# Softmax attention of a hybrid trunk on transposed scores, with the row maximum carried in a 65th row of the operand

## The chip, the cores and the metric

The kernel runs on one core of one Trainium2 chip. Its engines are TensorE (matrix products; PE in the profile, its weight loads PEld), VectorE (DVE), ScalarE (ACT), GpSimd (POOL) and SyncE (SP, which issues the loads of the weights). The metric is the device time of one execution in microseconds; the time of a kernel is the median of its runs.

## What is computed

Two trunk layers work on 512 latent tokens and 256 context tokens of width 1024, in f32. Each layer projects the normalised tokens, feeds three groups of heads (mean pooling, bidirectional gated linear attention, softmax attention), concatenates their outputs, projects them, and ends in a squared-ReLU MLP. The change touches only the softmax attention:

```python
def gqa_attend(qb, k, v):
    s = jnp.einsum('bqhgd,bkhd->bhgqk', qb, k, preferred_element_type=jnp.float32) * HEAD_DIM ** -0.5
    p = jax.nn.softmax(s, axis=-1)
    return jnp.einsum('bhgqk,bkhd->bqhgd', p.astype(v.dtype), v)
...
    k_all = jnp.concatenate([kc_, kl], axis=1)
    v_all = jnp.concatenate([vc_, vl], axis=1)
```

There are 8 query heads of 64 and 2 key/value heads, each shared by 4 query heads. Latent queries see all 768 keys (256 of the context, 512 latent); context queries see the 256 context keys. In the second layer the context is not updated, so only the latent queries are computed there.

## The kernel before

**Formats.** A matrix is held as two parts, hi and lo, in a reduced f32 format (F32R); products add hi*hi, hi*lo and lo*hi. The attention's probabilities and values are multiplied in plain f32, which the trace shows as two matmul instructions for each matmul of the program.

**Order of the work.** The kernel is written with generators ("threads"): `gla_thread` for the gated linear attention, `a_thread` for the projections, `mods` for the modulation and `att_thread` for the softmax attention. The string STEPS says for each layer in which order they are advanced, one letter for a step (g, a, m, t); at a t the projections and the modulation are first run to their ends. After the string, `gla_thread` and then `att_thread` are run out. A planner then orders each engine's instructions by its own estimate of times, in which an instruction that stands earlier goes first if it is ready. So each engine's order is fixed when the program is built, and an engine that waits keeps everything behind it waiting.

**Buffers.** `slot` gives one of 33 shared buffers [128, 768] in SBUF; the weights' pool `wp` has 3 buffers "raw", 5 "hi" and 5 "lo" of 1024 columns, which the attention also uses. PSUM: `psA` two buffers of two banks, `psB` three of one bank, `psC` one of one bank.

**The attention** (lines 928 to 1059). `k_stack` transposes the keys and stacks them per kv head: kh holds the hi part twice (rows 0 to 63 and 64 to 127), kl the lo part twice. `q_stack(hp)` transposes the queries of a pair of heads hp (four pairs) and holds per head qs, hi above lo. A unit is two query tiles of 128 of one pair. `softmax_part` makes, for each of the unit's four (head, tile) cases, scores with the queries on the partitions, [128 queries, 768 keys], from kh and kl (L974, L975), in a psA buffer; VectorE takes the negated maximum along the keys (L977), ScalarE the exponential with that as bias, and the sum with it (L978). `value_part` takes, for each of six key tiles, four transposes of p on TensorE (L992), a copy out of PSUM on ScalarE or VectorE (L996, L998), and the product with the values for two heads, 256 columns each (L1001), added up in psC. At its end a product with the identity spreads the reciprocal sums over the partitions (L1008), VectorE multiplies (L1014), and the hi and lo parts of the result go to mixT. Context queries are a third unit of each pair in layer 0. In `att_thread` a unit's value part is interleaved with the next unit's softmax part, and one step of `pool_thread` follows each unit.

## Time and profile before

| what | value |
|---|---|
| median of 3 runs | 1718.49 us (1718.38 to 1723.11) |
| span of the profiled execution (its own time) | 1719.9 us, 1.4 us over the median |
| TensorE busy | 1639.1 us, 95% |
| VectorE, ScalarE, GpSimd busy | 866.9, 656.9, 480.3 us |
| mean granted TensorE clock | 0.980 |
| attention in layer 0 / layer 1 | from 222 to 388 us / from 1179 to 1306 us of the span |

Times are from the start of the span. In a group or a step of the timeline, "out<-in" names the tiles; a bracket gives the idle time before and what ended it. In a table by stretches each engine has its busy time and in brackets its number of instructions; then come the granted clock, the busy share of the DMA engines and GB/s. The busy time of matmuls counts overlapping ones once, while the mean duration of one is longer than the distance at which matmuls follow each other; distances are therefore taken from starts.

### The profile page before, as it was taken

How to read it: one execution, taken by the hardware profiler on the slowest of the kernel's cores; microseconds unless marked ns; L12 is line 12 of the kernel's file. 1: busy time of each engine (PE TensorE's matmuls, PEld its weight loads, DVE VectorE, ACT ScalarE, POOL GpSimd, SP SyncE). 2: the span in 40 equal slices, each digit the busy share in tenths (PEclk: the TensorE clock that was granted, in tenths of full speed). 3: DMA queues.
4: the chain of work that ended last, by engine and by line, in shares of the span. 5: the costliest groups of instructions: out<-in, count | busy, mean ns of one | idle time of the engine just before them, and what ended most of it. 6: DMA issues, size and time to landing. Idle time of an engine off the chain costs nothing.

```text
span 1719.9 us, 28685 instructions
## 1 busy us (share of the span) xinstructions
PE 1639.1 (95%) x12059; PEld 1337.3 (78%) x12059; DVE 866.9 (50%) x1209; ACT 656.9 (38%) x1136; POOL 480.3 (28%) x514
## 2 busy tenths in 40 slices
PE   7999797999999999999999999898899999999997
PEld 4988655669987887877888888696568888888885
DVE  4447758643543334333353454767764555445554
ACT  5445356662432113122131134646663432222222
POOL 1104535202301220312313263244312212222225
PEclk9999899999999999999999999898999999999999
DMA  9422340203343415334131222200014233333331
GB/s 309 131 85 75 136 161 3 100 27 122 111 138 96 153 50 184 120 94 147 50 122 56 68 89 75 72 2 2 2 74 130 79 99 98 99 98 98 98 98 49
DMA packets 140256, 163.38 MB, mean 95 GB/s; under 512 B 9412, under 2 KB 116304, under 8 KB 140128
## 3 DMA queue, kind: packets, MB, share of 16 engines
q1 hardware_dynamic: 133312, 147.10, 26.9%
q10 hardware_dynamic: 6816, 14.46, 2.3%
q8 instruction: 94, 1.54, 0.4%
q14 instruction: 34, 0.28, 0.0%
HBM read 157.31 MB, written 4.23 MB: 94 GB/s over the span
## 4 chain that ended last, share of the span: by engine, by line
PE 85%; DVE 5%; POOL 3%; DMA 2%; ACT 2%; issue 2%; SPq 0%; ACTq 0%; POOLq 0%; DVEq 0%
PE dn L291 25%; PE up L272 19%; PE op L291 7%; PE tm L291 6%; PE up L274 5%; PE fm L272 4%; PE av L1001 3%; PE pT L992 2%; PE pm L175 2%; PE up L281 2%; PE fm L274 2%; DMA rawm<-in_w_mod_dram 1%; PE sc L974 1%; PE att L722 1%; PE sc L975 1%
## 5 line engine op out<-in xcount | busy, mean ns | idle before, releaser
L144 ACT ACTIVATE whi<-raw 128x1024 fp32r<-128x1024 f32 (+2 forms) x182 | 184.8, 1031 | 582.2 <-PE dn L291 310.3
L1131 POOL TENSOR_TENSOR X<-X,rtmp 128x512 f32<-128x512 f32 x158 | 218.0, 1384 | 660.9 <-DVE rtmp L1130 660.6
L68 DVE TENSOR_TENSOR wlo<-raw,whi 128x1024 fp32r<-128x1024 f32 (+2 forms) x182 | 225.5, 1247 | 279.0 <-ACT whi L144 273.7
L291 PE MATMUL dn<-whi,ah 128*128 128x512 f32 x640 | 249.8, 390 | 0.4 <-DVE rtmp L1130 0.4
L291 PE MATMUL dn<-whi,al 128*128 128x512 f32 x640 | 249.1, 389 | 0.0
L291 PE MATMUL dn<-wlo,ah 128*128 128x512 f32 x640 | 246.8, 389 | 0.0
L1130 DVE TENSOR_TENSOR rtmp<-dn,ga 128x512 f32<-128x512 f32 x160 | 109.2, 689 | 231.4 <-PE dn L291 229.8
L272 PE MATMUL up<-h2h,whi 128*128 128x512 f32 x464 | 183.8, 396 | 0.7 <-ACT relu L1173 0.7
L272 PE MATMUL up<-h2l,whi 128*128 128x512 f32 x464 | 182.5, 393 | 0.0
L272 PE MATMUL up<-h2h,wlo 128*128 128x512 f32 x464 | 182.5, 393 | 0.0
L291 PEld LDWEIGHTS dn<-whi,ah 128*128 128x128 f32 x640 | 120.1, 188 | 29.8 <-ACT whi L144 4.2
L291 PEld LDWEIGHTS dn<-wlo,ah 128*128 128x128 f32 x640 | 120.1, 188 | 25.0
L291 PEld LDWEIGHTS dn<-whi,al 128*128 128x128 f32 x640 | 120.1, 188 | 24.5
L272 PEld LDWEIGHTS up<-h2h,whi 128*128 128x128 f32 x464 | 87.1, 188 | 31.4 <-ACT relu L1173 7.6
L272 PEld LDWEIGHTS up<-h2l,whi 128*128 128x128 f32 x464 | 87.1, 188 | 21.1 <-issue 1.7
L291 PE MATMUL tm<-whi,hTh 128*128 128x256 f32 (+1 forms) x352 | 102.6, 292 | 0.0
L272 PEld LDWEIGHTS up<-h2h,wlo 128*128 128x128 f32 x464 | 87.1, 188 | 19.6
L291 PE MATMUL tm<-whi,hTl 128*128 128x256 f32 (+1 forms) x352 | 101.3, 288 | 0.0
L291 PE MATMUL tm<-wlo,hTh 128*128 128x256 f32 (+1 forms) x352 | 100.5, 287 | 0.0
L291 PE MATMUL op<-whi,mixh 128*128 128x256 f32 x320 | 91.2, 285 | 0.9 <-ACT whi L144 0.9
L291 PE MATMUL op<-wlo,mixh 128*128 128x256 f32 x320 | 90.2, 284 | 0.3 <-DVE wlo L68 0.3
L291 PE MATMUL op<-whi,mixl 128*128 128x256 f32 x320 | 90.5, 283 | 0.0
(287 smaller groups left out, 3318.7 us busy)
## 6 DMA issues: line engine op xcount, KB each, us to landing
rawm<-in_w_mod_dram SPq DMA_DIRECT2D x80, 512.0 KB
raw<-in_w_up_dram SPq DMA_DIRECT2D x64, 512.0 KB
raw<-in_w_down_dram SPq DMA_DIRECT2D x64, 512.0 KB
raw<-in_w_in_dram SPq DMA_DIRECT2D x26, 512.0 KB
rawm<-in_w_mod_dram SPq DMA_DIRECT2D x32, 256.0 KB
raw<-in_w_out_dram SPq DMA_DIRECT2D x16, 512.0 KB
raw<-in_w_in_dram SPq DMA_DIRECT2D x12, 256.0 KB
ga<-gaD ACTq DMA_DIRECT2D x6, 512.0 KB
```

The costliest lines, as they stand in the source:

```text
L68: V.tensor_tensor(lo, full, hi.bitcast(F32), ALU.subtract)
L144: A.activation(hi, raw, AF.Copy)
L175: T.matmul(pm[32 * j:32 * j + 32, :], sstat[:, k, :], raw[:, (j % 2) * 512:(j % 2) * 512 + 512], start=(k == 0), stop=(k == KT - 1), skip_ ...
L272: T.matmul(ps[:, 0:NL], a, b[:, 0:NL], start=st, stop=sp_)
L274: T.matmul(ps[:, NL:NT], a, b[:, NL:NT], start=st, stop=sp_)
L281: T.matmul(ps[:, cs], a, b[:, cs], start=(k == 0 and i == 0), stop=(k == nk - 1 and i == 2))
L291: T.matmul(ps, a[:, sl], bb, start=(k == 0 and i == 0), stop=(k == nk - 1 and i == 2))
L722: T.matmul(ps[g * bw:(g + 1) * bw, o0:o0 + bw], xk[rows, j0:j0 + bw], xq[rows, i0:i0 + bw], start=True, stop=True)
L992: T.transpose(pt_[:, i * 128:(i + 1) * 128], p_[:, ki * 128:(ki + 1) * 128], ident)
L1001: T.matmul(av_[64 * hh:64 * hh + 64, 0:256], vst, pe[:, hh * 256:hh * 256 + 256], start=(ki == 0), stop=(ki == len(kts) - 1))
L1130: V.tensor_tensor(tmp, ps, ga[0 if t < 4 else 1][:, sl], ALU.mult)
L1131: (V if b == NB - 1 and not both and t == 3 else G).tensor_tensor(X[t][:, sl], X[t][:, sl], tmp, ALU.add)
```

## The change

The scores are made transposed, with the keys on the partitions, [128 keys, 512 queries], so that the exponentials come out in the layout in which the product with the values takes them.

- `k_stack`: kl keeps the lo part in rows 0 to 63 and gets a row of ones as row 64.
- `max_part(hp)` replaces `q_stack`: per head qs (hi and lo; for the second head of a pair with the halves exchanged) and a second operand qm (the hi part in rows 0 to 63, copied by GpSimd). Then scores with the queries on the partitions are made once more, from the hi parts alone (64 rows), for the maximum of each query (VectorE); the maxima of a pair are transposed by a product with the identity and put as row 64 of qm by ScalarE.
- `scores`: kh times qs, plus the first 65 rows of kl times qm. The row of ones times the row of negated maxima subtracts the maximum within the product; the exponential needs no bias.
- `lat_part(hp)`: six key tiles by two heads, each 512 queries wide; exponential into p; the product with the values, 512 columns per head, one key tile behind, into psC. The sums over the keys: GpSimd adds the p tiles (two additions of 1024 columns per head), VectorE the two halves, and in `weigh` a product with a column of ones adds over the partitions.
- `weigh`: the reciprocal by Ln and Exp on ScalarE and one correction on VectorE, then the hi and lo parts.
- `ctx_part(hp)`: the same for the context queries, in layer 0.
- `att_thread`: `max_part` of the next pair is interleaved with the current pair's parts; two steps of `pool_thread` follow each pair. STEPS is as before.

Two constants are added at the start: the identity in F32R, and `nmx`, zeroed, for the maxima. Comments and docstrings are removed as well.

```diff
+    identr = const.tile([128, 128], F32R, name="identr")
+    V.tensor_copy(identr, ident)
+    nmx = const.tile([128, 6, 33], F32R, name="nmx")
+    A.activation(nmx, ident[:, 0:1].unsqueeze(1).to_broadcast([128, 6, 33]), AF.Copy, scale=0.0)
...
-                G.tensor_copy(kl[64:128], kl[0:64].bitcast(F32))
+                A.activation(kl[64:65], ident[64:65, 64:65].to_broadcast([1, NT]), AF.Copy)
...
-        def softmax_part(n, hp, q0, P):
-        def value_part(n, hp, q0, P):
-        def q_stack(hp):
+        def max_part(hp):
+            mix_new(4 + hp)
+            pq = [psB("qT"), psB("qT")] if both else [psB("qT")]
             for t in live:
                 T.transpose(pq[t // 4][:, (t % 4) * 128:(t % 4 + 1) * 128], qview(t, hp), ident)
             for hh in range(2):
+                qs, qm = slot("qs", F32R), slot("qm", F32R)
+                hr, lr = slice(64 * hh, 64 * hh + 64), slice(64 - 64 * hh, 128 - 64 * hh)
                 for i, pq_ in enumerate(pq):
                     n0, n1 = (0, NL) if i == 0 else (NL, NT)
+                    src = pq_[hr, 0:n1 - n0]
+                    A.activation(qs[hr, n0:n1], src, AF.Copy)
+                    sub_lo(qs[lr, n0:n1], src, qs[hr, n0:n1])
+                G.tensor_copy(qm[0:64, 0:N_], qs[hr, 0:N_].bitcast(F32))
+                qst[2 * hp + hh] = (qs, qm)
+            yield
+            kh = kst[hp // 2][0]
+            for t in lat_tiles:
+                ps = [psA("mx"), psA("mx")]
+                for z0, zn in ((0, NL), (NL, NC)):
+                    for hh in range(2):
+                        hr = slice(64 * hh, 64 * hh + 64)
+                        T.matmul(ps[hh][:, z0:z0 + zn], qst[2 * hp + hh][0][hr, t * 128:(t + 1) * 128],
+                                 kh[hr, z0:z0 + zn], start=True, stop=True)
+                for hh in range(2):
+                    V.tensor_reduce(nmx[:, t, 32 * hh:32 * hh + 1], ps[hh][:, 0:NT], AX.X, ALU.max, negate=True)
+                yield
...
+            ps = psA("mT")
+            for t in live:
+                T.matmul(ps[0:33, t * 128:(t + 1) * 128], nmx[:, t], identr, start=True, stop=True)
+            for hh in range(2):
+                r0 = 32 * hh
+                A.activation(qst[2 * hp + hh][1][64:65, 0:N_], ps[r0:r0 + 1, 0:N_], AF.Copy)
+            yield
+        def scores(ps, hp, hh, kt, q0, qn):
+            kh, kl = kst[hp // 2]
+            qs, qm = qst[2 * hp + hh]
+            ks = slice(kt * 128, (kt + 1) * 128)
+            T.matmul(ps, kh[:, ks], qs[:, q0:q0 + qn], start=True, stop=False)
+            T.matmul(ps, kl[0:65, ks], qm[0:65, q0:q0 + qn], start=False, stop=True)
+        def weigh(hp, av, acc, q0, n):
+            sm = psB("sum")[:, 0:n]
+            for hh in range(2):
+                T.matmul(sm[64 * hh:64 * hh + 64], one.to_broadcast([128, 64]), acc[hh], start=True, stop=True)
+            r, u = slot("r", w=512)[:, 0:n], slot("u", w=512)[:, 0:n]
+            A.activation(r, sm, AF.Ln)
+            A.activation(r, r, AF.Exp, scale=-1.0)
+            V.scalar_tensor_tensor(u, r, -1.0, sm, ALU.mult, ALU.mult)
+            V.tensor_tensor(r, av, r, ALU.mult)
+            V.scalar_tensor_tensor(r, u, 2.0, r, ALU.add, ALU.mult)
+            mhi, mlo = mixT[4 + hp]
+            A.activation(mhi[:, q0:q0 + n], r, AF.Copy)
+            G.tensor_tensor(mlo[:, q0:q0 + n], r, mhi[:, q0:q0 + n].bitcast(F32), ALU.subtract)
+        def lat_part(hp):
+            av = psC("av")
+            P, acc = {}, []
+            pend = []
+            for kt in range(6):
+                for hh in range(2):
+                    if kt % 2 == 0:
+                        P[hh, kt // 2] = wp.tile([128, 1024], F32, tag="lo" if hh else "hi", name=nm("p"))
+                    s_ = psB("sT")
+                    scores(s_, hp, hh, kt, 0, NL)
+                    p_ = P[hh, kt // 2][:, (kt % 2) * 512:(kt % 2) * 512 + 512]
+                    A.activation(p_, s_, AF.Exp)
+                    pend.append((hh, kt, p_))
+                for hh, k_, p_ in pend[:-2]:
+                    T.matmul(av[64 * hh:64 * hh + 64, :], vview(k_, hp // 2), p_, start=(k_ == 0), stop=False)
+                pend = pend[-2:]
+                if kt == 3:
+                    for hh in range(2):
+                        acc.append(wp.tile([128, 1024], F32, tag="raw", name=nm("acc"), bufs=3))
+                        G.tensor_tensor(acc[hh], P[hh, 0], P[hh, 1], ALU.add)
+                yield
+            for hh, k_, p_ in pend:
+                T.matmul(av[64 * hh:64 * hh + 64, :], vview(k_, hp // 2), p_, start=False, stop=True)
+            for hh in range(2):
+                G.tensor_tensor(acc[hh], acc[hh], P[hh, 2], ALU.add)
+                V.tensor_tensor(acc[hh][:, 0:512], acc[hh][:, 0:512], acc[hh][:, 512:1024], ALU.add)
+            yield
+            weigh(hp, av, [a_[:, 0:512] for a_ in acc], 0, NL)
+            yield
...
         def att_thread():
             k_stack()
             yield
+            yield from max_part(0)
+            for hp in range(4):
+                nxt = max_part(hp + 1) if hp < 3 else iter(())
+                for part in (lat_part(hp), ctx_part(hp) if both else iter(())):
+                    for _ in part:
+                        next(nxt, None)
+                        yield
+                for _ in nxt:
+                    yield
                 next(pool_, None)
+                next(pool_, None)
             run(pool_)
```

More of the change, by code (lines that the diff above doesn't have):

```diff
@@ L1028, in q_stack @@
             for hh in range(2):
-                qs = slot("qs", F32R)
+                qs, qm = slot("qs", F32R), slot("qm", F32R)
+                hr, lr = slice(64 * hh, 64 * hh + 64), slice(64 - 64 * hh, 128 - 64 * hh)
                 for i, pq_ in enumerate(pq):
                     n0, n1 = (0, NL) if i == 0 else (NL, NT)
-                    src = pq_[64 * hh:64 * hh + 64, 0:n1 - n0]
-                    A.activation(qs[0:64, n0:n1], src, AF.Copy)
-                    sub_lo(qs[64:128, n0:n1], src, qs[0:64, n0:n1])
@@ L1035, in q_stack @@
-                qst[hp * 2 + hh] = qs
+                    src = pq_[hr, 0:n1 - n0]
[15 more added lines that the diff above has]
+                yield
@@ new lines, in max_part @@
+            if both:
+                ps = psA("mx")
+                for i in range(2):
+                    for hh in range(2):
+                        hr = slice(64 * hh, 64 * hh + 64)
+                        T.matmul(ps[:, hh * 512 + i * NC:hh * 512 + (i + 1) * NC],
+                                 qst[2 * hp + hh][0][hr, NL + i * 128:NL + (i + 1) * 128], kh[hr, NL:NT],
+                                 start=True, stop=True)
+                V.tensor_reduce(nmx[:, 4:6, 0:33:32].rearrange("p t h -> p h t"),
+                                ps.rearrange("p (h t k) -> p h t k", h=2, t=2), AX.X, ALU.max, negate=True)
+                yield
@@ new lines, in lat_part @@
+        def lat_part(hp):
[21 more added lines that the diff above has]
+                T.matmul(av[64 * hh:64 * hh + 64, :], vview(k_, hp // 2), p_, start=False, stop=True)
+            for hh in range(2):
+                G.tensor_tensor(acc[hh], acc[hh], P[hh, 2], ALU.add)
[3 more added lines that the diff above has]
+            yield
@@ new lines, in ctx_part @@
+        def ctx_part(hp):
+            av = psC("avc")[:, 0:NC]
+            ps, acc = [], []
+            for hh in range(2):
+                s_ = psB("sTc")
+                for i in range(2):
+                    scores(s_[:, i * NC:(i + 1) * NC], hp, hh, 4 + i, NL, NC)
+                p_ = slot("pcx", w=512)
+                A.activation(p_, s_, AF.Exp)
+                ps.append(p_)
+            yield
+            for i in range(2):
+                for hh in range(2):
+                    T.matmul(av[64 * hh:64 * hh + 64, :], vview(4 + i, hp // 2), ps[hh][:, i * NC:(i + 1) * NC],
+                             start=(i == 0), stop=(i == 1))
+            for hh in range(2):
+                acc.append(slot("accx", w=NC))
+                G.tensor_tensor(acc[hh], ps[hh][:, 0:NC], ps[hh][:, NC:512], ALU.add)
+            weigh(hp, av, acc, NL, NC)
+            yield
@@ L1039, in att_thread @@
             yield
-            q_stack(0)
-            yield
-            nonlocal nunits
-            units = [(hp, q0) for hp in range(4) for q0 in ((0, 2, 4) if both else (0, 2))]
-            nunits = len(units)
-            prev = iter(())
-            for n, (hp, q0) in enumerate(units):
-                P = []
-                for i, _ in enumerate(softmax_part(n, hp, q0, P)):
-                    for _ in range(2 if i < 2 else 1):
-                        next(prev, None)
+            yield from max_part(0)
[4 more added lines that the diff above has]
+                        next(nxt, None)
+                        yield
+                for _ in nxt:
                     yield
-                run(prev)
-                if q0 == 0 and hp < 3:
-                    q_stack(hp + 1)
-                prev = value_part(n, hp, q0, P)
                 next(pool_, None)
-                yield
-            yield from prev
+                next(pool_, None)
             run(pool_)
```

68 lines of the change are left out of this document (removed).

## The prediction

> **What bounds the kernel now.** I read the page first, then the busy time by stage, then single steps of the attention on the timeline, then the chain of waits at the stage's ends. The page's rows:
>
> ```profile
> span 1719.9 us, 28685 instructions
> PE 1639.1 (95%) x12059; PEld 1337.3 (78%) x12059; DVE 866.9 (50%) x1209; ACT 656.9 (38%) x1136; POOL 480.3 (28%) x514
> PE 85%; DVE 5%; POOL 3%; DMA 2%; ACT 2%; issue 2%; SPq 0%; ACTq 0%; POOLq 0%; DVEq 0%
> ```
>
> TensorE holds 85% of the chain that ended last. The chain in order of time shows where the attention starts (the keys' transposes) and where the output projection takes over in layer 0, and the same in layer 1:
>
> ```profile
> 222.46 0.81 PE kT L933 x6
> ...
> 387.97 37.10 PE op L291 x307
> ...
> 1179.08 0.66 PE kT L933 x6
> ...
> 1305.35 14.71 PE op L291 x121
> ```
>
> Busy time in these two stages, and in three stretches of them where the linear attention (the GLA thread) runs beside:
>
> ```profile
> core 0: us, PE busy (x) PEld busy (x) DVE busy (x) ACT busy (x) POOL busy (x), PEclk, DMA share, GB/s
> 222.00:388.00 166.00, 148.40 (x1777) 98.54 (x1773) 106.39 (x175) 103.91 (x232) 55.29 (x74) 0.96 0.19 68
> 1179.00:1306.00 127.00, 113.56 (x1253) 77.45 (x1252) 85.53 (x134) 84.06 (x177) 38.83 (x55) 0.95 0.14 50
> ...
> 240.00:260.00 20.00, 16.52 (x239) 11.76 (x238) 17.06 (x28) 15.07 (x30) 9.99 (x11) 0.91 0.05 15
> 260.00:280.00 20.00, 13.82 (x348) 9.17 (x349) 18.68 (x23) 14.34 (x30) 16.21 (x18) 0.83 0.02 4
> 1200.00:1220.00 20.00, 18.11 (x340) 11.09 (x339) 19.69 (x31) 16.63 (x39) 15.37 (x22) 0.91 0.01 3
> ```
>
> Over both stages TensorE is the bound (148 of 166, 114 of 127 us), with 17.6 and 13.4 us idle. In the stretches with GLA it is VectorE (18.7 and 19.7 of 20 us), GpSimd is near behind, and TensorE idles at a granted clock of 0.83 to 0.91. How much of the old work lies behind GLA's end, the transposes of p show:
>
> ```profile
> 222.00:318.00 96.00, 12.46 (x72) 8.14 (x72) 3.38 (x5) 6.80 (x12) 0.93 0.16 58
> 318.00:388.00 70.00, 24.30 (x153) 16.41 (x152) 7.62 (x12) 16.25 (x28) 1.00 0.23 82
> ...
> 1255.00:1306.00 51.00, 18.15 (x120) 12.82 (x120) 6.89 (x10) 11.59 (x20) 1.00 0.34 121
> ```
>
> 153 of 225 in layer 0, so 68%, run after 318 us, and 120 of 192 (62%) in layer 1 after 1255 us; there GLA's matmuls have ended, and only TensorE's sum of work counts.
>
> **The change, priced on TensorE.** I count per pair of heads (four pairs a layer). A step of the old value part, from one group of four transposes to the next, and a tile of the old scores:
>
> ```profile
> 336.49 0.40 PE L974 MATMUL sc<-kh,qs 128*128 128x512 f32 x1
> 336.72 0.39 PE L975 MATMUL sc<-kl,qs 128*128 128x512 f32 x1
> 336.95 0.28 PE L974 MATMUL sc<-kh,qs 128*128 128x256 f32 x1
> 337.06 0.28 PE L975 MATMUL sc<-kl,qs 128*128 128x256 f32 x1
> ...
> 355.09 0.65 PE L1001 MATMUL av<-pe,UV 128*64 128x256 f32 x4
> 355.67 0.66 PE L992 MATMUL pT<-ident,p 128*128 128x128 f32 x4
> 356.26 0.65 PE L1001 MATMUL av<-pe,UV 128*64 128x256 f32 x4
> ...
> 381.56 0.61 PE L1008 MATMUL rb<-ident,sm 128*64 128x128 f32 x8
> 382.00 0.60 PE L1001 MATMUL av<-pe,UV 128*64 128x256 f32 x4
> ```
>
> I take starts, since durations overlap: a step is 356.26 - 355.09 = 1.17 us, of which 0.58 is the f32 product for 256 columns on both heads (the trace shows each f32 matmul as two instructions). A matmul of 512 columns in the scores takes 0.23, one of 256 takes 0.12, so a tile is 2 x 0.23 + 2 x 0.12 = 0.70 us. The reciprocal sums take 0.44 us a unit.
> *Before, latent:* 8 score tiles 5.6, 12 steps 14.0, two rb groups 0.9: 20.5 us. *Context (layer 0):* 8 matmuls of 256 1.0, 2 steps 2.3, rb 0.4: 3.7 us. Layer 0: 4 x 24.2 = 96.8; layer 1: 4 x 20.5 = 82.0.
>
> *After.* The nearest row to an f32 product with 512 columns on two heads is the modulation's pair of 512-column f32 matmuls:
>
> ```profile
> 237.05 1.05 PE L175 MATMUL pm<-rawm,sstat 128*32 128x512 f32 x4
> 238.03 0.43 PE L756 MATMUL o<-AT,GU 128*64 128x128 f32 x2
> ```
>
> It occupies 0.98 us. Bounds: 0.86 (the 0.58 scaled without its fixed part, about 2 x 0.43) and 1.16 (twice 0.58); I take 0.98, the same shape. So a key tile costs 4 score matmuls x 0.23 + 0.98 + 0.1 for the change between the two formats = 2.0 us, 12.0 for six. The pass for the maxima (max_part) multiplies 64 rows per head. GLA's 64-row matmuls in the chain:
>
> ```profile
> 210.42 1.54 PE att L722 x93
> ```
>
> They start every 1.54 / 93 = 0.017 us, so two heads can share the array, there with 32 to 64 columns. Bounds for a query tile: 0.35 (fully shared) and 0.70 (one after the other); I take 0.55, as 128-column weight loads come in any case: 2.2 for four tiles. Transposing the maxima (mT) is six matmuls of at most 0.11 (a transpose step is 0.58 / 4 = 0.15 with its change of format): 0.7, in layer 1 0.4. The sums by a product with ones: 0.98. Latent: 15.9 in layer 0, 15.6 in layer 1. Context: 8 x 0.12 + 2 x 0.58 + sum 0.58 + maxima 0.24 = 2.9. Layer 0: 4 x 18.8 = 75.2; layer 1: 62.4.
> **Sum on TensorE:** 178.8 - 137.6 = 41.2 us less. Queries are transposed as before.
>
> **The other engines.**
>
> ```profile
> L996 ACT ACTIVATE pe<-pT 128x512 f32<-128x512 f32 x72 | 41.5, 597 | 22.3 <-PE pT L992 18.4 <-PE av L1001 3.4
> L977 DVE TENSOR_REDUCE nmx<-sc 128x1 f32<-128x768 f32 x64 | 60.5, 953 | 25.9 <-PE sc L975 25.5
> L1130 DVE TENSOR_TENSOR rtmp<-dn,ga 128x512 f32<-128x512 f32 x160 | 109.2, 689 | 231.4 <-PE dn L291 229.8 <-POOL X L1131 1.7
> L925 POOL TENSOR_TENSOR mixl<-pm,mixh 128x768 fp32r<-128x768 f32 x2 | 3.6, 1817 | 7.8 <-ACT mixh L924 7.8
> L925 POOL TENSOR_TENSOR mixl<-pm,mixh 128x512 fp32r<-128x512 f32 x2 | 2.6, 1284 | 4.0 <-ACT mixh L924 4.0
> ```
>
> ScalarE: twelve exponentials of 512 columns at 0.6 (L996) are 7.2 us a pair; with split, row copies, Ln and Exp under 15 of TensorE's 16 to 19: hidden. The copies of transposed p (72 x 0.6) go. VectorE: the 8 reductions stay (7.6 us); 2.75 us of pe copies a pair go, three operations at 0.69 and two half-sums come: no gain, no loss. GpSimd: four sums of 128x1024 a pair. From 512 to 768 columns a sum grows by 0.53 us, so 1024 take 1.82 + 0.53 = 2.35; 9.4 us a pair, 75 us in all, where 55 and 39 us were busy. It stays below TensorE, so no term in throughput.
>
> *Waits that come.* The value product keeps its one bank until weigh has read it. After the last exponential of a pair come two GpSimd sums 4.7, VectorE 0.7, the ones product 1.0, Ln and Exp 1.2, two VectorE operations 1.4: 9.0 us. Queued behind is the next pair's first value product and, in order behind that, all of TensorE; ScalarE's exponentials and VectorE's maxima wait for TensorE. Cover: the old pair's last two products (2.0) and the next pair's scores, 12 x 0.46 = 5.5 us, which need only score banks and p tiles. That is 7.5, and max_part steps lie between, so I price it at nothing where the scheduler puts scores ahead; without that cover see the slower rival. The qm tiles double what a pair holds of the 33 shared buffers; if max_part then starts late, up to 8 reductions (7.6 us) stand open per pair: 0 to 46 us for the six hand-overs, and I take 0, as emission runs one pair ahead.
> *GLA.* GpSimd's operations are already stretched when VectorE is busy:
>
> ```profile
> 243.81 0.83 POOL L704 TENSOR_TENSOR xk<-b 128x384 f32<-128x384 f32 x1
> ...
> 261.66 1.71 POOL L697 TENSOR_TENSOR xq<-b 128x384 f32<-128x384 f32 x1
> ```
>
> STEPS, whose letters stay, issues 26 attention steps among GLA's in either layer. In layer 0 that was 26 of about 65 steps and is now 26 of about 48, so about two pairs' sums (18.8 us a layer) fall among such operations. Bounds 0 and 18.8; GpSimd was nearly full in one 20 us stretch of the five that GLA takes, so I take a fifth, 4 a layer: plus 8. The Trainium skill, "SBUF — State Buffer", section "Who interferes with whom", says that VectorE with two SBUF inputs and GpSimd reading SBUF block each other for a whole instruction; the factor of 2 in the two rows agrees. By that rule taken to its end the 18.8 would be lost whole in both layers, and the sum would be 1719.9 - 41.2 + 37.6 = 1716.3.
> *The ends.* No DMA is added or moved on its queue, but in layer 0 the first weight of the output projection waits for a raw buffer:
>
> ```profile
> 381.82 3.76 DMA raw<-in_w_out_dram
> ...
> 385.60 1.06 ACT whi L144
> ```
>
> Now two of the three raw buffers carry the sums and one is free early; against that stands the last pair's 9 us. Bounds -6 and +9 a layer; I take 0. The constants at the start (one 128x128 copy, one activation): 0 to 1, taken 0.
>
> Forecast: 1719.9 - 41.2 + 8 = 1686.7 for the profiled execution; the runs' median stands 1.4 lower, so **1685 us**.
>
> **Rivals.**
> 1. *Forecast*, chance 0.52, own range 1670 to 1703 (maxima unshared +5, GLA 0 to +20, ends).
> 2. *Idle time goes too*, 0.17: score banks are freed by one reduction instead of reduction and exponential, so GLA gets them sooner and half of the 31 us idle goes: 1719.9 - 41.2 - 15.5 = 1663, by the runs 1662. For it: the idle lies in the GLA stretches. Against: VectorE at 19.7 of 20 there.
> 3. *The saving falls into the GLA stretch*, 0.12: only what lies behind GLA counts (68% of 21.6, and 62% of 19.6: 26.8), and GpSimd's sums stretch GLA by two thirds of their 18.8, 13 a layer, which the rows with twofold times make possible: 1720 - 26.8 + 26 = 1719, by the runs 1718. For it: the two GpSimd rows. Against: TensorE's total would have to leave 40 us idle.
> 4. *Slower: the single value bank*, 0.19. If the order puts the next pair's first value product after only two key tiles (1.8 us) and the old products (2.0), 9.0 - 3.8 = 5.2 us stand open in each of eight pairs, 42 us: even. With the sums stretched twofold, as in the rows above, 4.7 becomes 9.4 and 9.9 x 8 = 79 us stand open: 1719.9 - 41.2 + 79 + 8 = 1766. Midway, 1745. It decides from 5 us a pair. For it: a bank without a second buffer, sums on the slowest engine. Against: the order of today's steps shows products and transposes of other units filling such waits.
>
> **How the numbers follow.** Within 0.3% (5 us) a measurement of this kernel cannot be told from no change. Faster: 0.52 + 0.17 + 0.03 of rival 3 = 0.72; same 0.08; slower 0.20. Range: 1656 leaves out the best part of rival 2, 1728 the worse two thirds of rival 4; 1685 is the likeliest.
>
> **What would show it.** Right: value products in steps of about 2.0 us a key tile, no transposes of p, the two stages about 18 and 16 us shorter. Wrong: TensorE waiting for VectorE's or GpSimd's sums ahead of the first value product of a pair (rival 4); GLA ending over 10 us later (rival 3); max_part's heads starting 0.23 us apart (the unshared bound); a key tile well over 2.0 us.

## The result, and the profile after

The changed kernel takes 1812.67 us (median of 4 runs, 1809.57 to 1819.27) where the kernel before, run beside it, takes 1720.8 us: a ratio of 1.0533, 95% interval 1.0504 to 1.0562, so about 92 us slower. Forecast was 1685 us with a range of 1656 to 1728. Neither the forecast nor its range held.

The page after (its span and its busy times):

```profile
span 1810.2 us, 27365 instructions
PE 1696.6 (94%) x11459; PEld 1312.0 (72%) x11459; DVE 889.2 (49%) x1190; ACT 629.9 (35%) x1025; POOL 563.2 (31%) x558
```

TensorE is *busier* than before (1696.6 against 1639.1 us) with 600 instructions fewer. The chain in order of time shows that the attention of layer 0 begins where it did, and that GLA's last matmuls (rg) and the output projection (op) come far later; then layer 1:

```profile
221.49 0.81 PE kT L939 x6
...
350.54 1.93 PE rg L787 x16
...
435.87 4.94 PE op L296 x31
...
1232.45 0.65 PE kT L939 x6
...
1346.90 1.02 PE rg L787 x16
```

Busy time by stretch, from the keys' transposes to the first matmul of the output projection in each layer (columns as in the prediction: length, busy PE, PEld, DVE, ACT, POOL, granted clock, DMA). First the kernel before, then the one after:

```profile
222.00:387.00 165.00, 147.68 (x1772) 98.03 (x1769) 105.39 (x174) 103.30 (x231) 55.29 (x74) 0.96 0.19 67
1179.00:1302.00 123.00, 109.56 (x1223) 74.08 (x1221) 82.52 (x131) 82.46 (x175) 38.83 (x55) 0.94 0.12 44
```

```profile
221.00:434.00 213.00, 175.54 (x1448) 82.38 (x1443) 117.91 (x164) 87.56 (x158) 98.15 (x97) 0.83 0.16 54
1232.00:1387.00 155.00, 131.64 (x938) 59.51 (x937) 89.76 (x117) 68.66 (x130) 76.34 (x73) 0.80 0.08 28
```

The two stretches grew from 165 + 123 = 288 to 213 + 155 = 368 us, so 80 of the 90 us by which the span grew lie here. No engine is full in them. I split a stretch into three parts that add up to it: *idle* is its length less PE busy; *clock loss* is (1 - granted clock) times its length, which is what half clock costs if TensorE is busy throughout it (an estimate); *work* is the rest, TensorE's work as it would be at full clock. Sums over both layers, in us (the clock's two digits leave about 2 us open):

| kernel | length | idle | clock loss | work |
|---|---|---|---|---|
| before | 288 | 31 | 14 | 243 |
| after | 368 | 61 | 67 | 240 |
| forecast for after (and 8 for GLA) | 255 | 31 | 14 | 202 |

So three things went wrong at once: the work fell by 3 us and not by 41, the idle time doubled, and the clock loss rose by 53 us.

Where the work stayed is seen in layer 0 behind GLA's end. The timeline of TensorE (start, duration):

```profile
373.70 0.50 PE L1004 MATMUL sT<-qs,kh 128*128 128x512 f32 x1
...
374.38 1.07 PE L1037 MATMUL av<-p,UV 128*64 128x512 f32 x2
375.38 0.50 PE L1004 MATMUL sT<-qs,kh 128*128 128x512 f32 x1
...
377.05 0.61 PE L975 MATMUL mx<-kh,qs 64*128 64x512 f32 x2
377.59 0.50 PE L1004 MATMUL sT<-qs,kh 128*128 128x512 f32 x1
...
387.02 0.62 PE L975 MATMUL mx<-kh,qs 64*128 64x512 f32 x4
...
398.29 0.29 PE L1005 MATMUL sTc<-qm,kl 65*128 65x256 f32 x1
...
404.25 2.03 PE L1066 MATMUL avc<-pcx,UV 128*64 128x256 f32 x7 [4.67 <-ACT pcx L1061]
...
414.73 1.08 PE L1037 MATMUL av<-p,UV 128*64 128x512 f32 x4
...
416.87 1.08 PE L1037 MATMUL av<-p,UV 128*64 128x512 f32 x4
```

"x4" is the product of both heads (two instructions each), "x2" that of one head. Both last the same: 1.08 and 1.07 us. A key tile with the heads side by side takes 416.87 - 414.73 = 2.14 us (forecast 2.0). With the heads apart one *head* takes 375.38 - 373.70 = 1.68 us, so 3.36 a tile. Counted in the trace's order, 37 of the 96 latent value products stand alone between other work. The maxima's products do the same: their rows last 0.62 us for two heads together (x4) and 0.61 us for one head alone (x2). By starts, one head alone takes 377.59 - 377.05 = 0.54 us, and both heads side by side take 0.55 us (1348.98 to 1349.53 us, in layer 1).

Where the idle time came from: TensorE's three largest waits in layer 0's stretch, 21 of its 37 us of idle time (engine, line, releaser: us in total, times, longest), and what ScalarE did around one of the first kind:

```profile
PE avc L1066 <- ACT pcx L1061: 11.8, 3, 6.9
PE mx L975 <- DVE nmx L978: 4.8, 6, 1.7
PE sum L1011 <- DVE acc L1048: 4.3, 1, 4.3
```

```profile
399.61 0.60 ACT L1014 ACTIVATE r<-sum 128x512 f32<-128x512 f32 x1 [4.10 <-PE sum L1011]
...
403.08 0.63 ACT L1020 ACTIVATE mixh<-r 128x512 fp32r<-128x512 f32 x1 [2.21 <-DVE r L1018]
403.61 1.06 ACT L1061 ACTIVATE pcx<-sTc 128x512 f32<-128x512 f32 x2
```

The context's scores (sTc) were ready at 398.6 us. Their exponentials (pcx) stood in ScalarE's queue behind the latent weigh of the same pair (Ln, Exp, mixh), which waited for the sums; so they began at 403.61, 5 us late, with ScalarE idle for most of that time. TensorE's context product (avc) waited for them from 399.6 to 404.25, and all behind it waited too.

The end of layer 1, where nothing is left to cover the last pair's chain:

```profile
1379.96 1.03 PE L1045 MATMUL av<-p,UV 128*64 128x512 f32 x4
1385.55 1.97 PE L1011 MATMUL sum<-acc,one 128*64 128x512 f32 x2 [4.56 <-DVE acc L1048]
1387.44 0.58 PE L296 MATMUL op<-whi,mixh 128*128 128x256 f32 x1
```

### The profile page after: what moved, and what is told of

Same layout as the page of the kernel before. It is cut to its first block, busy times and chain, and to the rows that moved or that the text cites. A ratio compares the mean times of both kernels' runs of the same rounds, so it can differ in the third digit from the quotient of the medians.

```text
span 1810.2 us, 27365 instructions
## 1 busy us (share of the span) xinstructions
PE 1696.6 (94%) x11459; PEld 1312.0 (72%) x11459; DVE 889.2 (49%) x1190; ACT 629.9 (35%) x1025; POOL 563.2 (31%) x558
## 4 chain that ended last, share of the span: by engine, by line
PE 82%; DVE 6%; issue 4%; ACT 3%; POOL 3%; DMA 2%; ACTq 0%; POOLq 0%; SPq 0%; DVEq 0%
PE dn L296 23%; PE up L277 18%; PE tm L296 6%; PE op L296 6%; PE up L279 5%; PE fm L277 4%; PE av L1037 3%; PE pm L180 2%; PE up L286 2%; PE sT L1004 2%; PE fm L279 1%; DMA rawm<-in_w_mod_dram 1%; PE mx L975 1%; PE sum L1011 1%; DVE nmx L978 1%
## 5 line engine op out<-in xcount | busy, mean ns | idle before, releaser
L68 DVE TENSOR_TENSOR wlo<-raw,whi 128x1024 fp32r<-128x1024 f32 (+2 forms) x182 | 230.4, 1274 | 286.9 <-ACT whi L149 283.7
```

Source lines behind the costliest of these rows:

```text
L68: V.tensor_tensor(lo, full, hi.bitcast(F32), ALU.subtract)
```

## The experiments

Four theories at the start. **P**: products of one head alone cost as much as those of two. **W**: the chain of sums and weigh, behind one value bank or in the queues. **M**: the pass for the maxima. **C**: work that uses half of the array halves the clock. Each time is the median of a variant's runs (two of most, four of e20, one of e7); the ratio is to the kernel before, run beside it on the same chip, with its 95% interval. Where two variants are compared by their medians, the intervals leave about 10 us open, and more where the text says so.

### Heads bound together; sums left out; maxima left out

e1_pairs:

```diff
-    T.matmul(av[64 * hh:64 * hh + 64, :], vview(k_, hp // 2), p_, start=(k_ == 0), stop=False)
+    last = behind(T.matmul(av[64 * hh:64 * hh + 64, :], vview(k_, hp // 2), p_, start=(k_ == 0),
+                           stop=False), last)
```

(`behind` only fixes the order in TensorE's queue; `last` begins as the last score product.)

> The arithmetic of the changed kernel; only the order is bound: in lat_part the first value product of a key tile has to stand behind the last score of the next key tile, and the second head's product behind the first head's, so that most of the 96 products of head 0 stand next to those of head 1 (in the changed kernel 52 of 96 do). Theory P (products that stand apart cost twice and bring more changes of format): 30 to 50 us faster than the changed kernel, with the value products' own time on TensorE falling from 76 towards 50 us. Theory W (the weigh chain behind one value bank): within 10 us of the changed kernel, since sums and bank are as they were. Theory M (the pass for the maxima): within 10 us too. Theory C (half clock brought on by products that use half of the array at a time): as P in time, and the time at a granted clock of 0.5 in the two attention stages falls well below the 136 us of the changed kernel.

e2_nogsum:

```diff
-G.tensor_tensor(acc[hh], P[hh, 0], P[hh, 1], ALU.add)
...
-G.tensor_tensor(acc[hh], acc[hh], P[hh, 2], ALU.add)
-V.tensor_tensor(acc[hh][:, 0:512], acc[hh][:, 0:512], acc[hh][:, 512:1024], ALU.add)
+V.tensor_tensor(acc[hh][:, 0:512], P[hh, 2][:, 0:512], P[hh, 2][:, 512:1024], ALU.add)
```

> Leaves out GpSimd's four 128x1024 sums of each latent pair of heads, so that the denominators hold two of six key tiles only; scores are divided by 8 in the exponential so that nothing overflows (same instructions). Theory W: the waits of the weigh chain shrink by the sums' 5 us or more per pair, eight pairs: about 40 us faster than the changed kernel, or more where GLA's GpSimd operations were stretched (the GLA end in layer 0 back by 15 us of its 37). Theories P, C and M: less than 10 us faster, since TensorE's products and their order stay.

e3_nomax: max_part keeps the queries' part; the loop of mx, nmx and mT goes, and

```diff
-A.activation(qst[2 * hp + hh][1][64:65, 0:N_], ps[r0:r0 + 1, 0:N_], AF.Copy)
+A.activation(qst[2 * hp + hh][1][64:65, 0:N_], ident[64:65, 0:1].to_broadcast([1, N_]), AF.Copy)
```

> Leaves out the whole pass for the maxima (its matmuls, VectorE's reductions and the transposes of the maxima); the 65th row is zero and scores are divided by 8 in the exponential, so that nothing overflows. The pass was forecast at 2.2 to 3.1 us a pair on TensorE, some 21 us in all. Theory M (the pass costs far more than that, by its waits on the two banks and VectorE, and at half clock): 50 us or more faster than the changed kernel. Theories P and W: 15 to 25 us faster, the forecast price.

e5_pairs_nomax, both of these edits:

> Both edits: no pass for the maxima (65th row zero, scores divided by 8 in the exponential) and the value products of the two heads bound together. Theory P and M together: the sum of the two gains, 80 us or more faster than the changed kernel, so faster than the kernel before. If pairing gains only because the pass for the maxima stands between the two products, the two gains overlap and this run is less than 10 us ahead of the run without maxima alone. Theory C: with no 64-row products left, granted clock near 1.0 in layer 0 after GLA's end.

| kernel | us | ratio | us against the changed kernel |
|---|---|---|---|
| e1_pairs | 1819.61 | 1.0556 (1.0511 to 1.0602) | +7 |
| e2_nogsum | 1773.54 | 1.0289 (1.0212 to 1.0366) | -39 |
| e3_nomax | 1778.88 | 1.0320 (1.0273 to 1.0367) | -34 |
| e5_pairs_nomax | 1782.48 | 1.0341 (1.0298 to 1.0383) | -30 |

```profile
224.00:435.00 211.00, 169.39 (x1430) 80.91 (x1427) 114.65 (x163) 87.59 (x157) 98.78 (x97) 0.81 0.16 55
1234.00:1398.00 164.00, 138.91 (x939) 64.77 (x937) 87.66 (x116) 68.89 (x130) 76.91 (x73) 0.72 0.08 27
```

These are e1's stretches. Its work fell by 18 us (240 to 222, by the same split), which confirms what theory P says of the price; yet idle rose to 67, clock loss to 86, and the time did not fall (the 7 us more cannot be told from none). So P's work is real, and TensorE's work does not set the end. Leaving out the sums gave W's 39 us, though GLA's end, counted from the keys' transposes, came back by 9 us only, not 15. M's 34 us lie between the two expectations. By e3's stretches TensorE's work fell by 40 us, where the prediction priced the pass at 23:

```profile
224.00:419.00 195.00, 154.75 (x1335) 74.22 (x1330) 94.46 (x128) 86.79 (x158) 102.85 (x97) 0.79 0.17 59
1216.00:1355.00 139.00, 107.50 (x859) 47.50 (x857) 70.00 (x84) 67.64 (x130) 79.48 (x73) 0.85 0.09 31
```

(idle 72, clock loss 62, work 200). In e5 the gains did not add; binding the heads gained nothing there either, and the clock did not come back to 1.0 as theory C had it (0.78 in both stretches).

### The bank, the sums and the clock

e6_free (weigh), e8_late (lat_part, weigh; the context likewise), e9_free_late (both):

```diff
+avs = slot("avs", w=512)[:, 0:n]
+A.activation(avs, av, AF.Copy)
```

```diff
-G.tensor_tensor(acc[hh], acc[hh], P[hh, 2], ALU.add)
 V.tensor_tensor(acc[hh][:, 0:512], acc[hh][:, 0:512], acc[hh][:, 512:1024], ALU.add)
+V.tensor_tensor(acc[hh][:, 0:512], acc[hh][:, 0:512], P[hh, 2][:, 0:512], ALU.add)
-weigh(hp, av, [a_[:, 0:512] for a_ in acc], 0, NL)
+weigh(hp, av, [(acc[hh][:, 0:512], P[hh, 2][:, 512:1024]) for hh in range(2)], 0, NL)
```

> The arithmetic of the changed kernel; weigh first copies the value product from its bank to a shared buffer (one ScalarE copy, 0.6 us, for latent and context each), so that the bank comes free about 1 us after the last product and not at the end of the chain of sums. Theory W-bank (the next product stands behind the held bank): TensorE's 11.8 us of waits of the context products in layer 0 go, and with them part of the half clock: 20 to 40 us faster than the changed kernel. Theory W-sums (the length of GpSimd's sums is the cost, wherever they end): less than 8 us. Theory P (products apart) and M (maxima): less than 8 us.

> The same result with other sums: only the last key tile is left to the end. GpSimd adds four key tiles as before, VectorE (two operations of 512 columns a head) the halves of that and the fifth tile, and the product with ones takes the rest in a second accumulating step (about 1 us of TensorE a pair); in the context the product with ones takes both tiles and GpSimd's sum goes. Theory W-sums: most of the 39 us that leaving out the sums gave, less 8 us of TensorE: 20 to 35 us faster than the changed kernel. Theory W-bank: 10 to 25 us, since the bank is held for a shorter time. Theories P and M: 8 us slower (TensorE's added steps).

> Both edits: the bank freed by a copy, and the late sums. If held bank and long sums are one and the same wait, the gains overlap and this run is within 8 us of the better of the two; if they are two costs, the gains add up, to 45 us or more below the changed kernel (1767 us or less).

e6: 1816.2 us (1.0534, 1.0504 to 1.0565), e8: 1802.88 us (1.0457, 1.0423 to 1.0491), e9: 1817.26 us (1.0541, 1.0510 to 1.0571). With the bank freed early, TensorE waits for the same exponentials as long as before (waits of e6, layer 0):

```profile
PE avc L1069 <- ACT pcx L1064: 12.2, 3, 7.2
```

The bank was not the wait that ended last: that part of theory W falls. Shorter sums (e8) gave 10 us, half of what theory W-sums asked for at least, and nothing together with the copies: e9 met neither of its two expectations; why not, no run shows.

e7_clock (the kernel before, and behind its last output):

```diff
+def val(hh):
+    mm(ps[64 * hh:64 * hh + 64, 512:1024], m32[:, 0:64], m32)
...
+for _ in range(28):
+    val(0)
...
+for _ in range(18):
+    mx(0)
+    full(2)
+    val(0)
...
+for _ in range(28):
+    val(0)
+    val(1)
```

> The kernel before with some 250 us of TensorE work behind its last output, issued back to back with no waits, so that each kind's granted clock can be read: whole-array matmuls of 512 columns (0.23 us each) around five stretches of about 28 us: one head's f32 value product over and over; one head's 64-row product as in the pass for the maxima; the mixture of the changed kernel (64-row product, two whole-array ones, one head's value product); both heads' value products in turn; both heads' 64-row products in turn. Theory C (half of the array in use at a time is enough to halve the clock): granted clock near 0.5 in the first three stretches, near 1.0 in the last two and in the whole-array stretches. Rival (only waits of TensorE halve it): near 1.0 in all of them, one head's value product about 1.0 us, 64-row products 0.23 us apart.

The timeline of TensorE, with rows run together where the operation stays the same; then busy time and granted clock: one row near the start, and one each within the stretches of one head's value products, of 64-row products (with whole-array ones around) and of the mixture:

```profile
1716.49 23.53 PE L1213 MATMUL mic<-mr 128*128 128x512 f32 x90 [8.10 <-ACT mr L1208]
1739.95 24.25 PE L1213 MATMUL mic<-m 128*64 128x512 f32 x56
...
1818.03 1.07 PE L1213 MATMUL mic<-m 128*64 128x512 f32 x2
...
1820.11 1.07 PE L1213 MATMUL mic<-m 128*64 128x512 f32 x2
...
1868.33 24.25 PE L1213 MATMUL mic<-m 128*64 128x512 f32 x112
```

```profile
1720.00:1730.00 10.00, 10.00 (x40) 8.10 (x39) 0.00 (x0) 0.00 (x0) 0.00 (x0) 0.87 0.00 0
...
1740.00:1763.00 23.00, 23.00 (x55) 7.40 (x55) 0.00 (x0) 0.00 (x0) 0.00 (x0) 1.00 0.00 1
1765.00:1818.00 53.00, 53.00 (x231) 42.27 (x229) 0.00 (x0) 0.00 (x0) 0.00 (x0) 1.00 0.00 1
1819.00:1853.00 34.00, 34.00 (x83) 11.08 (x83) 0.00 (x0) 0.00 (x0) 0.00 (x0) 1.00 0.00 0
```

Theory C falls as it was stated: with no waits the clock stays at 1.00 in one head's value products, in 64-row products and in their mixture. Half clock follows waits: after 8.1 us without work TensorE started at half clock. But e7 enters each of these stretches at full clock, so it does not test a weaker form of C: that such work is slow to lift a clock that has fallen. No run tests that. A stretch of the kernel after speaks for it: behind a wait of 3.62 us the clock stayed at 0.50 for 22 us in which TensorE was busy throughout.

```profile
263.93 0.66 PE L957 MATMUL qT<-ident,Uq 128*128 128x128 f32 x2 [3.62 <-ACT p L1034]
```

```profile
265.00:287.00 22.00, 22.00 (x163) 8.24 (x162) 11.36 (x12) 9.83 (x22) 10.90 (x9) 0.50 0.00 1
```

In the traces' record the clock changes only at steps of 3.41 us. Counted there, over both stretches: of the steps at half clock in which TensorE was busy throughout, full clock followed on 5 of 5 in the kernel before, but on 10 of 23 in the kernel after.

Theory P's price is confirmed in the cleanest form: 28 value products of one head take 24.2 us (x56, 0.86 us each), and 28 of *two* heads take the same 24.2 us (x112). The mixture shows what it costs to change between these products, in format and in the part of the array that they use: a cycle (one value product, one 64-row product, two whole-array ones) takes 1820.11 - 1818.03 = 2.08 us, where its parts alone are 0.86 + 3 x 0.23 = 1.55, so 0.53 a cycle.

### The order of emission

e11_defer: a pair's context scores come first, the value products are copied out of their bank, and weigh is called late:

```diff
+avs = held(av, NL)
...
-weigh(hp, av, [a_[:, 0:512] for a_ in acc], 0, NL)
+left.append(lambda: weigh(hp, avs, [a_[:, 0:512] for a_ in acc], 0, NL))
...
+if kt in (1, 3) and left:
+    left.pop(0)()
```

> The same arithmetic and the same GpSimd sums in another order of emission: a pair's context scores and exponentials come ahead of its latent ones, its context product and a copy of it (0.6 us) behind the first latent tile, and weigh (sums product, Ln, Exp, normalising) of a pair is emitted only behind the second key tile of the next pair. Theory W-order (the chain's steps stand in the engines' in-order queues ahead of work that is ready: in the changed kernel the context's exponentials waited on ScalarE behind the latent weigh, and TensorE behind those): the waits of 4 to 7 us per pair behind GLA's end go, and with them half clock; 30 to 50 us faster than the changed kernel. Theory P (the lone products and changes of format fill TensorE): less than 10 us. Theory G (the attention's steps among GLA's stretch GLA, and that sets the end): less than 15 us.

e12_half_t: every second t of STEPS left out from the third on.

> The changed kernel with 14 instead of 26 attention steps issued among GLA's in each layer (every second letter t left out; the rest follows behind GLA). Theory G: GLA's end comes back by 20 us or more of its 37 in layer 0 and its 39 in layer 1, and the whole is 15 to 40 us faster than the changed kernel. Theory W-order: GLA's end comes back, but what is moved behind GLA meets the same waits; within 10 us of the changed kernel, or slower by up to 20.

e13_defer_late is e11 with e8's sums; e14_defer_late_half is that with e12's STEPS.

> The deferred order of the run before last and the late sums (GpSimd adds four key tiles, VectorE the fifth, the product with ones takes the last in a second step). Theory W-order: with the weigh chain out of the way, GpSimd's sums have no one waiting for them, so within 8 us of the deferred order alone. If GpSimd's sums cost by their share of GLA's GpSimd work or VectorE's: 10 us or more faster than the deferred order alone.

> Deferred order, late sums, and 14 attention steps among GLA's. If theory G holds beside W-order: 15 us or more faster than deferred order with late sums. If the two waits were one: within 8 us of it, or slower.

e11: 1794.08 us (1.0425, 1.0370 to 1.0480); e12: 1841.7 (1.0702, 1.0645 to 1.0759); e13: 1791.81 (1.0412, 1.0339 to 1.0485); e14: 1805.79 (1.0493, 1.0436 to 1.0550). The stretches of e13:

```profile
224.00:422.00 198.00, 175.43 (x1471) 81.34 (x1467) 118.00 (x172) 89.87 (x166) 75.49 (x84) 0.88 0.15 53
1218.00:1371.00 153.00, 134.93 (x948) 59.03 (x946) 92.96 (x123) 69.08 (x132) 59.07 (x65) 0.81 0.07 25
```

Deferring gives 19 us (its interval does not touch the changed kernel's), below the 30 to 50 expected; late sums on top give nothing that can be told. In e13 idle fell from 61 to 41 us and the clock loss from 67 to 53. Theory G falls: in e12 GLA ends even earlier than before the change (its last transposes of layer 0):

```profile
311.69 2.83 PE L784 MATMUL rg<-ident,rsg 128*64 128x128 f32 x24
```

that is at 314.5 us, against 352.5 by the chain's row of the changed kernel and 316.4 by the row below of the kernel before, and yet the kernel is 29 us *slower* than the changed one, more than any theory allowed.

```profile
314.84 1.53 PE L782 MATMUL rg<-ident,rsg 128*64 128x128 f32 x24
```

GLA's late end is a mark of attention work that now lies among GLA's, not a loss of its own. With the deferred order it is the same: e14 is 14 us slower than e13.

### Side by side, with the waits out of the way

e15_defer_late_pairs is e13 with e1's binding, also for sums and context products; e16_defer_late_mx gives the maxima of both heads one pair of banks:

```diff
-ps = [psA("mx"), psA("mx")]
+ps = psA("mx")
...
+    T.matmul(ps[:, hh * 512:hh * 512 + 512], qst[2 * hp + hh][0][hr, (t0 + i) * 128:(t0 + i + 1) * 128],
+             kh[hr, 0:NL], start=True, stop=True)
+V.tensor_reduce(loc[:, 0, i], ps.rearrange("p (h k) -> p h k", h=2), AX.X, ALU.max, negate=True)
```

e17_all has both.

> Deferred order and late sums, and the two heads' value products, context products and sums products bound next to each other. Theory P+W (the waits hid the price of lone products; with the waits gone TensorE's work sets the end behind GLA): value products on TensorE fall from 84 to about 55 us and the kernel is 15 to 35 us faster than deferred order with late sums (1757 to 1777 us). Theory L (the loop of scores, exponential and value product is bound by latency between engines, not by TensorE's work): within 8 us of 1792 us, with TensorE's idle time or half clock up by what its work fell.

> Deferred order and late sums, and another layout of the maxima: both heads' latent scores of a query tile in one pair of banks, the context columns of two query tiles in another, so that the heads' products stand side by side (three VectorE reductions of 1024 columns and one tiny minimum instead of four reductions of 768). Theory P+W: 64-row products take about half of their present 54 us, 10 to 25 us faster than deferred order with late sums. Theory L: within 8 us.

> Both. Theory P+W: the gains add, 30 to 55 us faster than deferred order with late sums, 1737 to 1762 us; near the kernel before but not clearly under it. Theory L: within 12 us of 1792 us.

e15: 1787.05 us (1.0379, 1.0256 to 1.0502), e16: 1787.93 (1.0384, 1.0291 to 1.0478): neither can be told from e13, and e15's interval is too wide to decide between its two theories. e17: 1774.73 (1.0308, 1.0247 to 1.0368), 17 us under e13, between the two expectations; the two intervals overlap. The stretches of e17:

```profile
224.00:404.00 180.00, 155.28 (x1483) 76.27 (x1479) 119.62 (x172) 89.01 (x166) 78.36 (x84) 0.90 0.16 59
1200.00:1347.00 147.00, 119.47 (x945) 54.56 (x943) 95.68 (x122) 69.33 (x132) 61.74 (x65) 0.83 0.07 26
```

Work fell by 26 us from e13 (257 to 232) and clock loss by 10, while idle rose by 12.

### More load on TensorE, and the best order without maxima

e18_filler (the changed kernel) and e19_all_filler (e17):

```diff
+T.matmul(ps, kh[:, ks], qs[:, q0:q0 + qn], start=True, stop=True)
 T.matmul(ps, kh[:, ks], qs[:, q0:q0 + qn], start=True, stop=False)
```

> The changed kernel with the first product of every score tile issued twice (the second overwrites the first): 96 more matmuls of 512 columns at 0.23 us and 16 of 256 at 0.12 us, 24 us of TensorE at full clock, 48 at half. Theory T (TensorE's sum of work sets the end): 24 to 48 us slower than the changed kernel. Theory K (half clock lengthens the path, and more load lifts the clock): half clock in the two stages falls from 136 us by 40 or more, and the time is within 10 us of the changed kernel or under it. Theory L (latency between engines sets the end, the clock does not matter): within 15 us, with half clock as it was.

> The same doubling on the deferred, paired kernel, where TensorE waits least. Theory T: 24 to 40 us slower than that kernel's 1775. Theory K: within 8 us of it, half clock well below its 89 us. Theory L: within 12 us, half clock as it was.

e18: 1817.55 us (1.0549, 1.0499 to 1.0598); e19: 1784.94 (1.0360, 1.0312 to 1.0407). The stretches of e18:

```profile
222.00:441.00 219.00, 184.12 (x1500) 95.05 (x1496) 121.32 (x164) 88.44 (x158) 96.61 (x97) 0.84 0.16 54
1241.00:1395.00 154.00, 132.53 (x986) 64.59 (x984) 89.46 (x117) 68.84 (x130) 74.54 (x73) 0.88 0.08 28
```

For 24 us of added work the split gives 263 - 240 = 23, so it measures what it should. The time rose by 5 us only: clock loss fell by 14 and idle by 4. Theory T falls for the changed kernel. Between K and L this does not decide: the half-clock time fell by 27 us (twice 14), short of K's 40, and did not stay as L has it. In e19 the cost is 10 us, which cannot be told from e18's 5; T's 24 to 40 us did not come. Its work rose by 20 us, idle fell by 6 and clock loss rose by 5, to 95 us of half clock, so K does not hold there; L's bounds do.

e20_all_nomax is e17 without the pass, as in e3.

> The deferred, paired kernel with late sums without the pass for the maxima (its products, reductions and transposes; 65th row zero, scores divided by 8 in the exponential). Priced as predicted, some 23 us on TensorE: 1750 to 1758 us. Theory M (the reductions and the bank pairs they hold cost as much again, as waits of TensorE among GLA's work): 1720 to 1740 us, level with the kernel before. Theory L (other waits take their place): 1762 us or more.

e20: 1739.97 us (1.0083, 1.0056 to 1.0111), 35 us under e17 and at the edge of what theory M expected. Its stretches, in which TensorE's work is 191 us:

```profile
222.00:395.00 173.00, 142.97 (x1362) 69.63 (x1360) 95.14 (x135) 88.20 (x165) 82.43 (x84) 0.82 0.16 58
1189.00:1315.00 126.00, 101.44 (x869) 46.70 (x867) 72.08 (x90) 68.87 (x132) 63.08 (x65) 0.82 0.08 30
```

That is 52 us less work than the kernel before, and still a stretch of 299 us against 288, since idle (55) and clock loss (54) are 64 us more than before the change (45).

| kernel | length | idle | clock loss | work |
|---|---|---|---|---|
| e1, heads bound | 375 | 67 | 86 | 222 |
| e2, no sums on GpSimd | 339 | 44 | 46 | 249 |
| e13, deferred, late sums | 351 | 41 | 53 | 257 |
| e17, and side by side | 327 | 52 | 43 | 232 |
| e20, and no maxima | 299 | 55 | 54 | 191 |
| e18, after with filler | 373 | 56 | 54 | 263 |
| e19, e17 with filler | 345 | 46 | 48 | 251 |

## Why the prediction was wrong

**"Over both stages TensorE is the bound."** This was right for the kernel before and was carried over to the kernel after, as the sum "1719.9 - 41.2 + 8" does. It is the step that failed first. e1 took 18 us of work off and e18 put 23 us on, and the time rose by 7 and by 5 us, neither of which can be told from no change. My reading, which no run tests, is that the mass of small independent steps of two units (transposes, copies, products) hid TensorE's waits before, and that the change took just these away. Idle rose by 30 us and clock loss by 53, both forecast at nothing.

**"So a key tile costs 4 score matmuls x 0.23 + 0.98 + 0.1".** The size was right for heads side by side (2.14). What failed is the silent assumption that they are: the program issues a head's product as soon as its exponential is there, and the row I priced by (the modulation's 0.98 us for four instructions) gave the price of two heads, without my asking what one alone takes. It takes the same (0.86 and 0.86 in e7), with a change on either side: 0.53 us a cycle in e7, where I had 0.1 a key tile. Price: at least the 18 us of work that e1 removed.

**"I take 0.55" for a query tile of the maxima,** with bounds 0.35 and 0.70. Side by side it is 0.55, as taken; apart it is 2 x 0.54 = 1.08, beyond the upper bound, since a head alone takes as long as two. Here too the silent assumption failed, not the size. In all the pass costs 40 us of TensorE's work (e3) and 34 to 35 us of time (e3, e20), for 23 predicted. These two terms are 18 + 17, about 35 of the 38 us that were missing from the saving.

**"I price it at nothing where the scheduler puts scores ahead"** (the weigh chain). GpSimd's sums were priced well: 2.35 us each, and two take 4.64 (row in the last section). But the chain is longer than I counted: VectorE's half-sum of a pair's first head was lengthened from 0.68 to 2.83 us (same fence; 2.8 us in five of the eight pairs), and the context's exponentials stood behind the chain on ScalarE. I named what is queued on TensorE alone, and looked for the next pair's products; late were the same pair's context products. With the sums left out 39 us go (e2), with the chain deferred 19 (e11).

**The ends,** "bounds -6 and +9 a layer; I take 0". In layer 1 the last value product ends at 1381.0 and the output projection starts at 1387.4, at half clock: 6 us, in the upper half of the bounds. In the kernel before, the projection of layer 1 started 3 us before the last value product ended.

**GLA, plus 8.** It ended 37 and 39 us later after the keys' transposes than before, far beyond the 8, yet e12 shows that this is where work was put.

**The rivals.** *Idle time goes too* was the reverse of what happened. *The saving falls into the GLA stretch* had its sign (GLA late) without its cause. *The single value bank* had the right side and chance 0.19, and names the sums on GpSimd rightly; its mechanism, the bank, was not the wait that ended last (e6), and its 1745 us fell 68 us short, since it kept the saving of 41 us. Of the signs listed, late GLA, TensorE waiting for sums and a key tile well over 2.0 us (apart) were all seen; of the signs of being right, the key tile held side by side alone, and the stretches grew by 48 and 32 us instead of shrinking by 18 and 16; no transposes of p remained, as forecast.

**What stays open.** Part of the 92 us is settled by removal: 21 for the order of weigh with late sums (e13), 17 for side by side (e17, whose interval overlaps e13's), 35 for the pass (e20, necessary work of which 23 was forecast); 15 us remain over the 1724.5 us measured beside e20, with all of it gone. Why idle time and clock loss stay at some 100 us in each of these is not shown, nor how much of the clock loss is a cause and how much only marks waits, nor whether one head's products and 64-row products kept the clock low once a wait had lowered it. By the count used at e7, half clock stayed on after a fully busy step 13 of 23 times in the changed kernel, 5 of 16 in e18, whose added products use the whole array, and 3 of 13 in e17, which fits; but 16 of 28 in e1, where most value products stand side by side, does not. Parts do not simply add: bound heads gave nothing on the changed kernel, and e9 lost what e8 gained. No version tried beats the kernel before.

## What to carry to other kernels

A sum of work taken off the busiest engine is a saving only as long as that engine stays the bound: ask what independent work the removed steps gave it to fill its waits, and work out the longest chain between engines for the kernel *after*. For two products that share an array, price both cases, side by side and alone, and look in the order of issue which one it will be. And for a chain with five stops, list what stands ahead of each stop in each in-order queue, not only on the main engine.

## What the hardware showed beside this

The price of waiting is paid twice. In e7 TensorE had no work for 8.1 us, began at 1716.49 and was granted full speed only from 1722.6 on (0.87 of the 10 us from 1720 are 2.6 us at half, if the rest is at full): 6.1 us of work at half speed. The Trainium skill, "TensorE: Matmul & The Clock Gate", Part 1 ("The HAM clock gate"), has the clock fall after an idle window of about 3.4 us and rise after one busy window; e7 and the wait of 3.62 us shown with it agree with the cause of the fall. For the rise, the 6.1 us of whole-array work in e7 are under two such windows, but in the kernel after 22 us of full work did not bring it; there the measurement decides.

VectorE's half-sum beside GpSimd, and alone (timeline of the kernel after, end of layer 1):

```profile
1380.30 4.64 POOL L1047 TENSOR_TENSOR acc<-acc,p 128x1024 f32<-128x1024 f32 x2
...
1382.66 2.83 DVE L1048 TENSOR_TENSOR acc<-acc 128x512 f32<-128x512 f32 x1 [3.46 <-POOL acc L1047]
1386.55 0.68 DVE L1048 TENSOR_TENSOR acc<-acc 128x512 f32<-128x512 f32 x1
```

The same operation takes 2.83 us while GpSimd's second sum runs, ending 0.55 us after GpSimd's end (1384.94), and 0.68 us alone. The prediction weighed this block as a loss for GpSimd; here GpSimd keeps its 2.32 us an operation and VectorE, which is in the weigh chain, pays. The Trainium skill, "SBUF — State Buffer", "Who interferes with whom", says that a VectorE instruction with two SBUF inputs contends with a GpSimd instruction that reads SBUF, and that the order of issue decides who is blocked; this row agrees.
